# Unread products of constants on TensorE, where it stands idle at the heads of stages, in two routers and behind a recurrence

## The chip, the core and the metric

The kernel runs on one core of a Trainium2 chip. The core has a matrix engine (TensorE, written PE in the profile, with PEld for its weight loads), a vector engine (VectorE, DVE), an activation engine (ScalarE, ACT), GpSimd (POOL) and a queue engine (SyncE, SP) that issues most transfers from the chip's main memory. The metric is device time of one execution in microseconds (us); a kernel's time is the median of its runs. TensorE's clock has two levels, 1.2 and 2.4 GHz; the profile gives the level granted in a stretch as a share of the full one (0.50 and 1.00).

## The reference

A network of eight stages works on 256 tokens of width 1024 (and, in the first three stages, on 256 more of a context), all in 32-bit floats:

```
l0   even_mixer: state-space scan + convolution branch, over 512 rows
m0   moe over 512 rows: sigmoid(t @ router_w), best group of 4 experts, best 2 in it,
     sum over experts of weight * (silu(t @ wg) * (t @ wu)) @ wd
hg   odd_mixer: gated linear recurrence in both directions, then rmsnorm * silu(gate), @ w_out
m1   moe over 256 rows
f0   rmsnorm, ffn: (silu(h @ w_gate) * (h @ w_up)) @ w_down
hy   hybrid of attention and a second gated recurrence
f1   two ffn
nsa  sparse attention
f3   ffn, final rmsnorm
```

In stages l0 to m1 the norm of each stage's input is scaled and shifted by `modulation(cond) = silu(cond) @ w + b`; from f0 on it has a gain alone. The change touches nothing that is computed: what it adds is written to a bank of PSUM that nothing reads.

## The kernel before

**Products.** Every matrix product with weights is made of three TensorE products on halves of the operands (`mm3`, L289 to L291): high by high, high by low, low by high. The weights come from memory as f32 (L456); ScalarE writes their rounded high half (L497), VectorE the rest (L498). A product of unrounded f32 operands ("plain f32") is one instruction in the program and two records in the trace.

**Head of a stage.** The rows are tokens, 128 to a tile. `normed` makes the root mean square from the sums of squares (L315, L333, then three Newton steps at L296 to L300) and scales the rows, even tiles on ScalarE (L379), odd ones on VectorE (L377). `turn` then transposes them on TensorE, 128 columns at a time (L392, one record each), into PSUM banks that VectorE (L413, L399) and ScalarE (L411, L398) empty, and the halves are made there too (L415, L416). Then come the stage's first L289. While the norm is made, TensorE has nothing to do. In f0, hy, f1, nsa and f3 the gain can be put in later, so that `turn` works on the rows before they are scaled; these six heads (f1 has two) are short.

**Router.** The turned rows are multiplied by the router's columns (L1156, then L1161 gathers the parts), ScalarE takes a tanh (L1163), and VectorE ranks the experts in some twenty small instructions, down to the mask of the chosen ones (L1190). TensorE counts each token's place in its expert with a triangle of ones (L1208 to L1210); VectorE makes rows of zeros and ones from the places (L1346 in m0, L1494 in m1), and TensorE turns these into lists of token numbers (m0: L1349, on which a gather by DMA and its transposes at L1363 follow) or multiplies with them (m1: L1501). In m0 TensorE also transposes the rows back for the gather's source (L1284); ScalarE (L1288) and VectorE (L1286) copy them.

**Between m0 and hg.** The last experts' outputs are sent back to their tokens by products (L1456), a bank each; VectorE takes each bank times a gate (L1458) and adds it to the row (L1459), eight times; ScalarE squares the rows (L315), and the head of hg begins.

**End of hg.** After the last products of the gate's projection come eight products of the modulation (L582), which need their weights alone. The last of the recurrence's results are normed and multiplied by the gate on VectorE (L1695), turned (L392), and multiplied by the output weights.

**First stage.** `first_parts` transposes all rows (L680), then the modulation's first part (L562, L567) gives scale and shift, which ScalarE and VectorE apply (L693) ahead of the first L289.

**What sets the order.** The program is traced once; a scheduler in the framework puts each engine's instructions in one list, by the traced order shifted by priorities (`high_priority`, offset up to 9 times `PRIO` = 3000) and by added edges (`issue_after`). Each engine then runs its list in order; an instruction whose operand or bank isn't ready holds all those behind it on its engine. PSUM banks come from pools that a stage opens (`banks=`): a new tile waits until the last reader of the bank that it gets is done, also when that reader belongs to the stage before.

Of the kernel before, what the change touches and what calls it, by code (L numbers as in the profile page):

```python
# [24 lines left out]
P = 128  # L25
# [38 lines left out]
HALF_HY = 5  # L64

# [113 lines left out]
class Ctx:  # L179
# [106 lines left out]
    def mm3(self, out, a, b, first, last):  # L286

        nc = self.nc
        nc.tensor.matmul(out, a[0], b[0], start=first, stop=False)  # L289
        nc.tensor.matmul(out, a[0], b[1], start=False, stop=False)  # L290
        nc.tensor.matmul(out, a[1], b[0], start=False, stop=last)  # L291
# [91 lines left out]
    def turn(self, xn, segs, hi, lo, full=None, of=0):  # L383
# [5 lines left out]
        for k in range(xn[0].shape[1] // P):  # L389
            ps = self.bank(of)  # L390
            for t in range(len(xn)):
                nc.tensor.transpose(ps[:, t * P:(t + 1) * P], xn[t][:, k * P:(k + 1) * P], self.ident)  # L392
# [258 lines left out]
def even_mixer(S, l, gains, X):  # L651
# [19 lines left out]
    with S.tc.manual_schedule(engines={nc.tensor.engine, nc.scalar.engine, V.engine}):  # L671
# [15 lines left out]
        next(firsts[1])  # L687
        for k, wh, wl in collect(W, KT):
            V.tensor_scalar(sc[:, :, k], S.mcol[0][:, 0, k], 1.0, gains[:, k:k + 1], op0=OP.add, op1=OP.mult)
            c, v, sh = plain[k][:, 0:256], plain[k][:, 256:512], S.mcol[0][:, 1, k]  # L690
            nc.scalar.activation(c, c, AF.Identity, scale=sc[:, 1, k:k + 1], bias=sh[:, 1:2])
            V.tensor_scalar(v, v, sc[:, 0, k:k + 1], sh[:, 0:1], op0=OP.mult, op1=OP.add)
            last = nc.scalar.activation(hT[0][k], plain[k], AF.Copy), V.tensor_sub(hT[1][k], plain[k], hT[0][k].bitcast(FT))  # L693
            for f in range(4):
                if f == BEF[k > 0]:
                    for g in firsts[k + 2:k + 3] + firsts[k + 1:k + 2]:
                        next(g)
                fs = slice(f * P, (f + 1) * P)
                S.mm3(four[f], (wh[:, fs], wl[:, fs]), (hT[0][k], hT[1][k]), k == 0, k == KT - 1)
# [444 lines left out]
def route(S, w, hf, nt, room):  # L1144
# [18 lines left out]
    scored = nc.scalar.activation(sc, ps[:, :nt * 16].rearrange("p (t e) -> p t e", e=16), AF.Tanh, scale=0.5)  # L1163
    sel = T("r_sel", nt, 4, 4)
# [45 lines left out]
    nc.tensor.matmul(ps[:, 64:80], S.ones, past[:, nt], start=False, stop=True)  # L1210
# [49 lines left out]
def route_all(S, w, X, segs, room):  # L1260
# [3 lines left out]
    nt = len(X)  # L1264
    xn = S.normed(X, w, known=True)
# [11 lines left out]
    else:  # L1277
        H = S.dram_pool.tile([nt * P, D], FT, name="tokens")
        for t in range(nt):
            h = S.page()  # L1280
            for q in range(2):
                ps = S.bank(1)
                for k in range(4):
                    nc.tensor.transpose(ps[:, k * P:(k + 1) * P], hf[4 * q + k][:, t * P:(t + 1) * P], S.ident)  # L1284
# [4 lines left out]
            nc.gpsimd.dma_start(H[t * P:(t + 1) * P], h)  # L1289
    return hf, H, aux, pos, sc, count  # L1290
# [34 lines left out]
def moe_wide(S, X, segs, gates):  # L1325
# [6 lines left out]
    with ExitStack() as st:  # L1332
# [117 lines left out]
        for t in range(nt):  # L1450
            for q in range(2):
                v = slice(q * 512, q * 512 + 512)
                b = S.bank(1 if t < 2 else 0)
                for i in range(2):
                    for j, y in enumerate(ys[i]):
                        nc.tensor.matmul(b, back[i][:, t * P:(t + 1) * P], y[:, v], start=i + j == 0, stop=i + j == 2)  # L1456
# [19 lines left out]
def moe_narrow(S, X, scale, shift, gates, beside):  # L1476
# [5 lines left out]
    with ExitStack() as st:  # L1482
# [58 lines left out]
        def down(e, act, a, back):  # L1541
# [15 lines left out]
            for t in range(nt):  # L1557
                for j in range(2):
                    for h, r in enumerate((lo, hi)):
                        nc.tensor.matmul(sums[t][h], back[r, t * P:(t + 1) * P], y[j][r], start=e + j == 0, stop=e == 15 and j == 1)  # L1560
# [63 lines left out]
def odd_mixer(S, xin, sc, sh):  # L1624
# [5 lines left out]
    hT = [Rows(S, 8, 512, FR) for _ in range(2)]  # L1630
    S.norm_T(xin, [(0, 2, sc[:, 1], sh[:, 1], None), (2, 2, sc[:, 0], sh[:, 0], "to")], *hT, known=True)
# [51 lines left out]
    for q in range(2):  # L1683
# [6 lines left out]
        if q == 0 and not ORDER:  # L1690
            recur(*last)
    oT = [Rows(S, 8, 256, FR) for _ in range(2)]
# [103 lines left out]
def ffn(S, xs, g, idx, first=None):  # L1796
# [6 lines left out]
    with ExitStack() as st:  # L1803
        w = S.work("ffn", st)
        if first:
# [3 lines left out]
            g = both  # L1809
        S.turn(xs, [(0, nt, g, None, None)], *hT)  # L1810
        if first:
# [101 lines left out]
def hybrid_mixer(S, x, g, name):  # L1913
# [5 lines left out]
    hT = [Rows(S, 8, 256, FR) for _ in range(2)]  # L1919
    S.turn(x, [(0, 2, g, None, None)], *hT)  # L1920
    rr = S.rstd(w, x)
# [239 lines left out]
def sparse_mixer(S, x, g, name):  # L2161
# [6 lines left out]
    hT = [Rows(S, 8, 256, FR) for _ in range(2)]  # L2168
    S.turn(x, [(0, 2, g, None, None)], *hT)
    rr = S.rstd(w, x)  # L2170
# [387 lines left out]
```

## Time and profile before

| | us |
|---|---|
| median of three runs | 2569.3 (2567.41 to 2569.53) |
| the profiled execution | 2571.33 |
| its span, first to last instruction | 2569.5 |
| TensorE busy in the span | 2391.0 (93%) |
| VectorE, ScalarE busy | 1566.4 (61%), 1264.5 (49%) |
| mean granted clock of TensorE | 0.968 |

The profile's page gives busy time by engine, the span in 40 slices with the granted clock, and the chain of waits that ended last. Three views of the trace are used beside it: the timeline (start, duration, engine, line, operation, operands, number of records; in brackets the idle time ahead of them and what ended it), the table of stretches (busy time and number of records of each engine between two moments, with the granted clock), and the granted clock of the whole span. Records of products on TensorE overlap, so that a product's pace is read from one start to the next, not from its duration.

### The profile page before, as it was taken

How to read it: one execution, taken by the hardware profiler on the slowest of the kernel's cores; microseconds unless marked ns; L12 is line 12 of the kernel's file. 1: busy time of each engine (PE TensorE's matmuls, PEld its weight loads, DVE VectorE, ACT ScalarE, POOL GpSimd, SP SyncE). 2: the span in 40 equal slices, each digit the busy share in tenths (PEclk: the TensorE clock that was granted, in tenths of full speed). 3: DMA queues.
4: the chain of work that ended last, by engine and by line, in shares of the span. 5: the costliest groups of instructions: out<-in, count | busy, mean ns of one | idle time of the engine just before them, and what ended most of it. 6: DMA issues, size and time to landing. Idle time of an engine off the chain costs nothing.

```text
span 2569.5 us, 31206 instructions
## 1 busy us (share of the span) xinstructions
PE 2391.0 (93%) x11991; PEld 1744.9 (68%) x11991; DVE 1566.4 (61%) x2519; ACT 1264.5 (49%) x2020; POOL 87.8 (3%) x103
## 2 busy tenths in 40 slices
PE   7999999889999599987999899998999999989998
PEld 5677776666666477765433478776788787756786
DVE  4999997678888826674111455456555554655554
ACT  5358654357777435553211344365444444546442
POOL 0000000011210300000000000000000000000000
PEclk9999999989999799998999999999999999989999
DMA  6552243479999444346999755333555553402552
GB/s 264 193 202 99 83 144 118 163 255 332 364 362 351 155 150 162 116 167 253 381 376 420 292 176 176 123 123 138 190 180 180 180 180 139 171 23 85 206 177 81
DMA packets 78054, 509.48 MB, mean 198 GB/s; under 512 B 9776, under 2 KB 10412, under 8 KB 21571
## 3 DMA queue, kind: packets, MB, share of 16 engines
q1 hardware_dynamic: 73603, 494.13, 52.5%
q0 software_dynamic: 4288, 13.21, 1.6%
q8 instruction: 97, 1.59, 0.2%
q14 instruction: 66, 0.54, 0.1%
HBM read 496.18 MB, written 12.87 MB: 198 GB/s over the span
## 4 chain that ended last, share of the span: by engine, by line
PE 46%; DVE 4%; ACT 3%; issue 1%; DVEq 0%; ACTq 0%
PE ps L289 11%; PE ps L291 11%; PE ps L290 11%; PE ps L1535 5%; PE ps L1552 2%; DVE wl L498 1%; PE ps L1831 1%; ACT wh L497 1%; DVE a L1828 1%; PE ps L1501 1%; PE ps L2281 1%; PE ps L1560 1%; PE ps L2317 0%; ACT pg L2292 0%; DVE ey L1555 0%
## 5 line engine op out<-in xcount | busy, mean ns | idle before, releaser
L498 DVE TENSOR_TENSOR wl<-raw,wh 128x1024 fp32r<-128x1024 f32 x618 | 748.7, 1224 | 497.8 <-ACT wh L497 494.4
L497 ACT ACTIVATE wh<-raw 128x1024 fp32r<-128x1024 f32 x618 | 640.4, 1053 | 576.9 <-PE ps L291 477.6
L289 PE MATMUL ps<-wh,pg 128*128 128x512 f32 (+2 forms) x1596 | 620.0, 389 | 17.4 <-DVE pg L399 6.1
L290 PE MATMUL ps<-wl,pg 128*128 128x512 f32 (+2 forms) x1596 | 613.9, 385 | 1.2 <-DVE wl L498 1.2
L291 PE MATMUL ps<-wh,pg 128*128 128x512 f32 (+2 forms) x1596 | 614.2, 385 | 0.0
L289 PEld LDWEIGHTS ps<-wh,pg 128*128 128x128 f32 x1596 | 303.0, 190 | 84.0 <-DVE pg L399 7.4
L291 PEld LDWEIGHTS ps<-wh,pg 128*128 128x128 f32 x1596 | 303.3, 190 | 62.3 <-issue 4.6
L290 PEld LDWEIGHTS ps<-wl,pg 128*128 128x128 f32 x1596 | 303.6, 190 | 58.9 <-DVE wl L498 2.1
L289 PE MATMUL ps<-pg,wh 128*128 128x512 f32 (+3 forms) x528 | 205.2, 389 | 2.9 <-ACT pg L693 2.9
L290 PE MATMUL ps<-pg,wh 128*128 128x512 f32 (+3 forms) x528 | 201.1, 381 | 0.5 <-DVE pg L693 0.5
L291 PE MATMUL ps<-pg,wl 128*128 128x512 f32 (+3 forms) x528 | 201.3, 381 | 0.0
L823 DVE SCALAR_TENSOR_TENSOR x<-pg,vecs,x 128x512 f32<-128x512 f32 x240 | 171.6, 748 | 2.6 <-ACT x L808 0.4
L1535 PE MATMUL ps<-raw,pg 128*64 128x512 f32 x512 | 131.6, 606 | 0.0
L289 PEld LDWEIGHTS ps<-pg,wh 128*128 128x128 f32 (+2 forms) x528 | 98.4, 186 | 42.0 <-issue 13.8
L291 PEld LDWEIGHTS ps<-pg,wl 128*128 128x128 f32 (+2 forms) x528 | 98.5, 187 | 22.5 <-issue 3.5
L290 PEld LDWEIGHTS ps<-pg,wh 128*128 128x128 f32 (+2 forms) x528 | 98.6, 187 | 19.1 <-DVE pg L693 1.1
L290 PE MATMUL ps<-wl,xe 128*96 128x512 f32 x256 | 104.3, 407 | 1.2 <-DVE wl L498 1.2
L289 PE MATMUL ps<-wh,xe 128*96 128x512 f32 x256 | 102.6, 401 | 0.0
L291 PE MATMUL ps<-wh,xe 128*96 128x512 f32 x256 | 102.5, 400 | 0.0
L1538 DVE TENSOR_TENSOR act<-act,ps 64x512 f32<-64x512 f32 x16 | 10.9, 679 | 128.9 <-ACT act L1537 128.9
L1535 PEld LDWEIGHTS ps<-raw,pg 128*64 128x64 f32 x512 | 38.4, 139 | 65.1 <-issue 62.7
L1552 PE MATMUL ps<-raw,eT 128*64 128x512 f32 x256 | 69.5, 596 | 0.0
(609 smaller groups left out, 2839.3 us busy)
## 6 DMA issues: line engine op xcount, KB each, us to landing
raw<-in_moe_w_up SPq DMA_DIRECT2D x64, 1024.0 KB, 7.4
raw<-in_moe_w_gate SPq DMA_DIRECT2D x64, 1024.0 KB, 8.6
raw<-in_moe_w_down SPq DMA_DIRECT2D x64, 1024.0 KB, 7.9
raw<-in_ffn_w_gate SPq DMA_DIRECT2D x44, 1024.0 KB, 5.0
raw<-in_ffn_w_up SPq DMA_DIRECT2D x44, 1024.0 KB, 4.9
raw<-in_ffn_w_down SPq DMA_DIRECT2D x44, 1024.0 KB, 4.9
raw<-in_mod_w SPq DMA_DIRECT2D x40, 1024.0 KB, 4.8
raw<-in_ab_w_in SPq DMA_DIRECT2D x20, 1024.0 KB, 5.0
```

Of the source, the lines that this page charges most:

```text
L289: nc.tensor.matmul(out, a[0], b[0], start=first, stop=False)
L290: nc.tensor.matmul(out, a[0], b[1], start=False, stop=False)
L291: nc.tensor.matmul(out, a[1], b[0], start=False, stop=last)
L497: nc.scalar.activation(hv, r, AF.Copy)
L498: nc.vector.tensor_sub(lv, r, hv.bitcast(FT))
L823: V.scalar_tensor_tensor(y3, u[:, :, j:j + 64], cfw[:, c, j:j + 1], y3, op0=OP.mult, op1=OP.add)
L1501: nc.tensor.matmul(ps[:, k * 256:(k + 1) * 256], H[i // nt][t][:, (2 * q + k) * P:(2 * q + k + 1) * P], p[:, t, :, 0], start=i == 0, stop= ...
L1535: nc.tensor.matmul(b[r], xe[kk][:, sv], W[:, k * 512:k * 512 + 512], start=kk == 0, stop=kk == KT - 1)
L1552: nc.tensor.matmul(b[r], aT[:, k], W[:, k * 512:k * 512 + 512], start=k == 0, stop=k == 3)
L1560: nc.tensor.matmul(sums[t][h], back[r, t * P:(t + 1) * P], y[j][r], start=e + j == 0, stop=e == 15 and j == 1)
L1828: V.scalar_tensor_tensor(a, up[t][:, :cn], r[t], a, op0=OP.mult, op1=OP.mult)
L1831: nc.tensor.transpose(ps[:, f * P:(f + 1) * P], a[:, f * P:(f + 1) * P], S.ident)
```

## The change

A helper `warm(n)` issues n plain f32 products of two constant tables, 128x128 by 128x256, into a PSUM bank that nothing reads. An edge puts them behind a given TensorE instruction (`behind`, or the last of the helpers that now note it in `self.last`), a priority ahead of the rest. It is called at the heads of m0 (20 products), hg (60), m1 (22) and the six short heads (3 ahead of the transposes, 6 behind them), behind the routers' first products (24 and 18), behind the counts (4 and 6), and at the end of hg ahead of its transposes (25). Nine more are written out in the first stage. That makes 242 products.

```
+WARM = {("head", 4): 20, ("route", 4): 24, ("placed", 4): 4, "hg": 60, "hg end": 25, ("head", 2): 22, ("route", 2): 18, ("placed", 2): 6, "ffn": 3,
+        "turned": 6}
...
-        nc.tensor.matmul(out, a[1], b[0], start=False, stop=last)
+        self.last = nc.tensor.matmul(out, a[1], b[0], start=False, stop=last)
+
+    def warm(self, n, of=0, behind=None):
+        if not n:
+            return
+        ps, ones = self.bank(of), self.squares[:, 1:3].rearrange("p i c -> p (i c)")
+        with self.tc.high_priority(offset=PRIO), self.tc.issue_after((behind or self.last).ins):
+            for _ in range(n):
+                self.nc.tensor.matmul(ps[:, :256], self.ident, ones, start=True, stop=True)
...
         next(firsts[1])
+        ps = S.bank(1)
+        for _ in range(9):
+            nc.tensor.matmul(ps[:, :256], S.ident, S.squares[:, 1:3].rearrange("p i c -> p (i c)"), start=True, stop=True)
         for k, wh, wl in collect(W, KT):
...
     scored = nc.scalar.activation(sc, ps[:, :nt * 16].rearrange("p (t e) -> p t e", e=16), AF.Tanh, scale=0.5)
+    if nt == 2:
+        S.warm(WARM["route", nt], behind=found)
...
-    nc.tensor.matmul(ps[:, 64:80], S.ones, past[:, nt], start=False, stop=True)
+    S.warm(WARM["placed", nt], behind=nc.tensor.matmul(ps[:, 64:80], S.ones, past[:, nt], start=False, stop=True))
...
     nt = len(X)
+    S.warm(WARM["head", nt])
     xn = S.normed(X, w, known=True)
...
             nc.gpsimd.dma_start(H[t * P:(t + 1) * P], h)
+        S.warm(WARM["route", nt], 1)
...
     hT = [Rows(S, 8, 512, FR) for _ in range(2)]
+    S.warm(WARM["hg"])
     S.norm_T(xin, [(0, 2, sc[:, 1], sh[:, 1], None), (2, 2, sc[:, 0], sh[:, 0], "to")], *hT, known=True)
...
             recur(*last)
+    S.warm(WARM["hg end"])
     oT = [Rows(S, 8, 256, FR) for _ in range(2)]
...
+        S.warm(WARM["ffn"])
         S.turn(xs, [(0, nt, g, None, None)], *hT)
+        S.warm(WARM["turned"])
```

The last hunk stands in `ffn` and, alike, in the stages hy and nsa. The transposes of `turn` and of the router, and the products that send rows back, note themselves in `S.last` too. The lines below the helper move by 12, later ones by 15 to 27: L392 is L404 after the change, L1284 L1302, L1208 L1225, L1456 L1475, L582 L594. The helper's product is L303.

TensorE's list from the last product of m0 to the head of hg. Before (`pg` are rows and parts of them, `ps` banks, `squares` the constant tables):

```order
L1456 MATMUL ps_10672<-pg_10537,pg_10357 128x512
L1456 MATMUL ps_10672<-pg_10538,pg_10357 128x512
L392 MATMUL ps_10746<-squares,pg_10734 128x128
L392 MATMUL ps_10746<-squares,pg_10735 128x128
L392 MATMUL ps_10746<-squares,pg_10736 128x128
```

and now:

```order
L1475 MATMUL ps_10733<-pg_10599,pg_10418 128x512
L303 MATMUL ps_10780<-squares 128x256 x60
L404 MATMUL ps_10868<-squares,pg_10856 128x128
L404 MATMUL ps_10868<-squares,pg_10857 128x128
L404 MATMUL ps_10868<-squares,pg_10858 128x128
```

The 60 products stand between the last L1475 (L1456 before) and the first of 32 transposes. The bank that they write, `ps_10780`, lies where the seventh of the eight banks of L1475, `ps_10723`, lay: the first of them waits until VectorE has read that one (L1477, L1458 before).

TensorE's list in the router of m0, from the last transposes back to the token lists. Before:

```order
L1284 MATMUL ps_4276<-squares,pg_4095 128x128 x2
L1284 MATMUL ps_4276<-squares,pg_4096 128x128 x2
L1208 MATMUL ps_4213<-r_mk_4195,squares 128x64
L1209 MATMUL ps_4213<-r_past_4207,ones 128x64
L1210 MATMUL ps_4213<-r_past_4207,ones 128x16
L1349 MATMUL ps_4288<-r_aux_4202,pe_4283 96x4 x4
```

and now:

```order
L1302 MATMUL ps_4312<-squares,pg_4126 128x128 x2
L1302 MATMUL ps_4312<-squares,pg_4127 128x128 x2
L303 MATMUL ps_4319<-squares 128x256 x24
L1225 MATMUL ps_4244<-r_mk_4226,squares 128x64
L1226 MATMUL ps_4244<-r_past_4238,ones 128x64
L1227 MATMUL ps_4244<-r_past_4238,ones 128x16
L303 MATMUL ps_4248<-squares 128x256 x4
L1368 MATMUL ps_4349<-r_aux_4233,pe_4344 96x4 x4
```

The 24 stand ahead of the counts, the four between the counts and the lists. The first of the 24 waits for a copy of ScalarE (L1306, L1288 before) out of the bank that it gets.

TensorE's list at the end of hg. Before:

```order
L291 MATMUL ps_12716<-wh_12769,pg_10718 128x512
L582 MATMUL ps_11942<-raw_12870,cond 32x512 x4
L582 MATMUL ps_11942<-raw_12876,cond 32x512 x4
L392 MATMUL ps_12829<-squares,pg_11103 128x128
L392 MATMUL ps_12834<-squares,pg_11103 128x128
L392 MATMUL ps_12839<-squares,pg_11103 128x128
```

and now:

```order
L293 MATMUL ps_12838<-wh_12891,pg_10779 128x512
L303 MATMUL ps_12911<-squares 128x256 x25
L404 MATMUL ps_12977<-squares,pg_11225 128x128
L404 MATMUL ps_12977<-squares,pg_11226 128x128
L404 MATMUL ps_12982<-squares,pg_11225 128x128
L404 MATMUL ps_12982<-squares,pg_11226 128x128
L404 MATMUL ps_12987<-squares,pg_11225 128x128
L404 MATMUL ps_12987<-squares,pg_11226 128x128
L404 MATMUL ps_12992<-squares,pg_11225 128x128
L404 MATMUL ps_12992<-squares,pg_11226 128x128
L594 MATMUL ps_12064<-raw_13018,cond 32x512
L404 MATMUL ps_12997<-squares,pg_11225 128x128
```

The 25 stand where the modulation's products stood, right behind the gate's projection; their bank's last reader is done by then. The eight products of the modulation (L594, L582 before) now stand among the transposes, one ahead of the ninth and the others behind the fourteenth and the sixteenth. The lists of GpSimd and SyncE are what they were; those of VectorE and ScalarE move one weight's halves in the router of m0.

## Rows read from the trace of the kernel before

**Rows 1.** Which engine is busy, and the granted clock in 40 slices (the page)
```profile
PE 2391.0 (93%) x11991; PEld 1744.9 (68%) x11991; DVE 1566.4 (61%) x2519; ACT 1264.5 (49%) x2020; POOL 87.8 (3%) x103
...
PEclk9999999989999799998999999999999999989999
```

**Rows 2.** The chain that ended last, by engine (the page)
```profile
PE 46%; DVE 4%; ACT 3%; issue 1%; DVEq 0%; ACTq 0%
```

**Rows 3.** Stretches of the span (the first line names the columns)
```profile
core 0: us, PE busy (x) PEld busy (x) DVE busy (x) ACT busy (x) POOL busy (x), PEclk, DMA share, GB/s
...
28.10:31.60 3.50, 3.50 (x15) 2.03 (x17) 0.69 (x1) 0.34 (x1) 0.00 (x0) 0.51 1.00 404
...
526.00:530.00 4.00, 4.00 (x10) 2.61 (x11) 1.05 (x3) 1.44 (x2) 0.72 (x1) 0.51 0.67 198
...
871.20:884.20 13.00, 0.00 (x0) 0.00 (x0) 12.33 (x37) 6.24 (x15) 0.00 (x0) 0.50 0.24 81
884.20:888.30 4.10, 4.05 (x18) 3.73 (x19) 2.65 (x7) 4.07 (x7) 0.00 (x0) 0.50 0.00 0
...
892.00:1138.00 246.00, 244.94 (x1462) 193.49 (x1460) 136.85 (x206) 125.22 (x186) 3.77 (x12) 1.00 0.39 142
...
1154.30:1158.00 3.70, 3.68 (x10) 2.91 (x11) 0.24 (x2) 0.27 (x1) 0.57 (x1) 0.51 1.01 418
...
1197.90:1205.70 7.80, 5.99 (x24) 5.14 (x26) 4.09 (x17) 1.78 (x4) 0.00 (x0) 0.50 0.03 6
```

**Rows 4.** Timeline of TensorE, a plain f32 product: start, busy us, line, shape, records, idle before
```profile
338.47 0.60 PE L1032 MATMUL ps<-pg,half 128*128 128x256 f32 x2
338.90 0.61 PE L1052 MATMUL ps<-pg,pg 128*128 128x128 f32 x4
```

**Rows 5.** Timeline around the head of hg
```profile
876.86 0.68 DVE L1458 TENSOR_TENSOR pg<-ps,pg 128x512 f32<-128x512 f32 x1
...
884.25 5.33 PE L392 MATMUL ps<-squares,pg 128*128 128x128 f32 x28 [16.69 <-ACT pg L379]
...
891.16 0.50 PE L289 MATMUL ps<-wh,pg 128*128 128x512 f32 x1 [0.71 <-ACT pg L411]
```

**Rows 6.** Timeline of TensorE, head and router of m0
```profile
488.06 0.28 PE L432 MATMUL ps<-squares,mcol 128*8 128x128 f32 x1 [1.11 <-DVE pg L783]
493.61 6.40 PE L392 MATMUL ps<-squares,pg 128*128 128x128 f32 x31 [5.27 <-ACT pg L379]
...
506.10 1.94 PE L1284 MATMUL ps<-squares,pg 128*128 128x128 f32 x16
514.35 0.69 PE L1208 MATMUL ps<-r_mk,squares 128*128 128x64 f32 x2 [6.30 <-DVE r_mk L1190]
...
518.64 2.35 PE L1349 MATMUL ps<-r_aux,pe 128*96 128x4 f32 x12 [1.43 <-DVE pe L1346]
...
524.34 1.51 PE L1363 MATMUL ps<-squares,xg 96*128 96x96 f32 x8 [1.58 <-DMA xg<-tokens,ix]
```

**Rows 7.** Timeline of TensorE, end of hg
```profile
1138.21 1.92 PE L582 MATMUL ps<-raw,cond 128*32 128x512 f32 x16
1146.70 1.12 PE L392 MATMUL ps<-squares,pg 128*128 128x128 f32 x4 [6.57 <-DVE pg L1695]
```

**Rows 8.** Timeline of TensorE, head and router of m1
```profile
1184.22 1.12 PE L392 MATMUL ps<-squares,pg 128*128 128x128 f32 x4 [6.13 <-ACT pg L379]
...
1197.93 0.61 PE L1208 MATMUL ps<-r_mk,squares 128*128 128x32 f32 x2 [4.84 <-DVE r_mk L1190]
...
1201.14 3.75 PE L1501 MATMUL ps<-pe,pg 128*128 128x256 f32 x16 [1.78 <-DVE pe L1494]
```

**Rows 9.** Timeline of TensorE, first stage
```profile
26.13 0.50 PE L289 MATMUL ps<-pg,wh 128*128 128x512 f32 x1 [2.54 <-ACT pg L693]
```

**Rows 10.** Stretches at two of the six small heads
```profile
1661.30:1666.50 5.20, 5.20 (x15) 4.78 (x16) 2.59 (x10) 2.76 (x8) 0.00 (x0) 0.50 0.34 102
1785.00:1787.00 2.00, 0.62 (x6) 0.39 (x5) 2.00 (x4) 2.00 (x7) 0.00 (x0) 1.00 0.00 0
```

More of the change, by code (lines that the diff above doesn't have):

```diff
@@ L391, in turn @@
             for t in range(len(xn)):
-                nc.tensor.transpose(ps[:, t * P:(t + 1) * P], xn[t][:, k * P:(k + 1) * P], self.ident)
+                self.last = nc.tensor.transpose(ps[:, t * P:(t + 1) * P], xn[t][:, k * P:(k + 1) * P], self.ident)
             if segs[0][3] is None and full is None:
@@ L1283, in route_all @@
                 for k in range(4):
-                    nc.tensor.transpose(ps[:, k * P:(k + 1) * P], hf[4 * q + k][:, t * P:(t + 1) * P], S.ident)
+                    S.last = nc.tensor.transpose(ps[:, k * P:(k + 1) * P], hf[4 * q + k][:, t * P:(t + 1) * P], S.ident)
                 if q:
@@ L1455, in moe_wide @@
                     for j, y in enumerate(ys[i]):
-                        nc.tensor.matmul(b, back[i][:, t * P:(t + 1) * P], y[:, v], start=i + j == 0, stop=i + j == 2)
+                        S.last = nc.tensor.matmul(b, back[i][:, t * P:(t + 1) * P], y[:, v], start=i + j == 0, stop=i + j == 2)
                 tmp = S.page()[:, :512]
@@ L1559, in down @@
                     for h, r in enumerate((lo, hi)):
-                        nc.tensor.matmul(sums[t][h], back[r, t * P:(t + 1) * P], y[j][r], start=e + j == 0, stop=e == 15 and j == 1)
+                        S.last = nc.tensor.matmul(sums[t][h], back[r, t * P:(t + 1) * P], y[j][r], start=e + j == 0, stop=e == 15 and j == 1)
             yield
@@ L1919, in hybrid_mixer @@
     hT = [Rows(S, 8, 256, FR) for _ in range(2)]
+    S.warm(WARM["ffn"])
     S.turn(x, [(0, 2, g, None, None)], *hT)
+    S.warm(WARM["turned"])
     rr = S.rstd(w, x)
@@ L2168, in sparse_mixer @@
     hT = [Rows(S, 8, 256, FR) for _ in range(2)]
+    S.warm(WARM["ffn"])
     S.turn(x, [(0, 2, g, None, None)], *hT)
+    S.warm(WARM["turned"])
     rr = S.rstd(w, x)
```

## The prediction

> **What bounds the kernel now.** I read the page first: TensorE is busy 93% of the span, and the clock line has four slices under 9 tenths [rows 1]. The chain that ended last gives TensorE 46% and every other engine 4% or less [rows 2]. So what shortens TensorE's list shortens the kernel, and what lengthens it lengthens it, except where it waits. Then the table of stretches, at the places of the change [rows 3]: the reader is to see that the clock is at 0.50 in stretches that follow an idle one, at the ends of gaps of 5 to 17 us, and that the 246 us of hg behind its head are full: 244.94 us busy at 1.00. Last the timelines of the heads and routers [rows 5 to 8], for when each gap ends and what ended it. With a mean clock of 0.968 some 3% of the span, 82 us, are lost to the half clock; but part of that is idle, and a good part lies where the change adds nothing.
>
> **The price of one unread product.** The same shape in the same type, 128*128 128x256 f32, stands at L1032: one product leaves two records, and from its start at 338.47 to the next start 0.43 us pass [rows 4]. Twice that, 0.86 us, at half the clock. The count of two records holds for plain f32 elsewhere: L1208 is one instruction in the list and two records [rows 6, 8]. So 242 products are 104 us of TensorE at full clock; each group is priced by where its start is held, its length, and when the next instruction is ready.
>
> **Head of hg (60).** The rows are ready for the transposes at 884.25, after 16.69 us idle. The products cannot start at the idle time's beginning: their bank is free when the seventh of eight gate products on VectorE is done, 876.86 + 0.68 = 877.54 [rows 5]. By then the clock is at 0.50 (from 871.20 on) [rows 3]. In the kernel before it rose 4.05 us after TensorE had set to work again (884.25 to 888.30); with the same lag 4.7 products run at 0.86 us and 55.3 at 0.43: 877.54 + 4.05 + 23.8 = 905.4. The transposes begin 21.1 us late. At full clock they win back at most half of 4.05 us; VectorE and ScalarE, which empty the banks, allow about 1.5. So +19.6 (18 to 21). Nothing behind swallows it: to 1138 TensorE is full [rows 3]. What it hides is small: the weights' halves get further ahead, and no wait for them is in the stretch. If the bank did not bind, the products would run from 867.56 (884.25 − 16.69) to 893.4, and the cost would be +7 to +9.
>
> Here the Trainium skill has a rule (TensorE: Matmul & The Clock Gate, Part 4: PE-mode transpose): the full clock does not engage for transposes, which do not count as busy. The rows differ: from 884.20 to 888.30 TensorE ran transposes alone, and the next stretch was at full clock. By the rule the first weight products of hg would have paid about 4 us at half clock before, the unread products would save 2 us more, and the sum would be some 2 us lower; the measurement decides, so I leave that out.
>
> **Head and router of m0 (20, 24, 4).** TensorE's last L432 starts at 488.06 [rows 6]; the products follow VectorE's read of a bank at about 488.6, and 20 × 0.43 end at 497.2, 3.6 us behind the transposes' old start of 493.61. These went at half clock, 31 in 6.3 us (0.20 each); at full clock L1284 has 16 in 1.94 (0.12) [rows 6], so 2.5 come back and the rest about comes back in the products behind: 0. The 24 begin when the transposes back (L1284, until about 508) and a copy out of their bank are done, and last 10.3 us, to about 518.3. The mask is ready for L1208 at 514.35: +4.0 there. Four more products stand ahead of L1349 (1.7 us, against an idle 1.43). Counts and lists run at full clock, so that L1349 is about 2 us late, and the gather, whose L1363 came at 524.34, with it. If the clock then holds over the wait for the gather, the stretch 526 to 530 (at 0.51) gives 2 us back; TensorE idles there once more, and in the idle time ahead of 884.25 the clock did fall, so that I count less than half. Sum +1.2 (−2 to +3).
>
> **End of hg (25).** These start when the gate's projection ends, at 1138.2, and end at 1148.9, 2.2 us behind the transposes' old start of 1146.70 [rows 7]. The 1.92 us of the modulation's products, which ran in that gap [rows 7], go among the transposes, where TensorE waits for banks. Against it the half clock to 1158 goes: 1154.3 to 1158 was full at 0.51 [rows 3], worth 1.8, and the transposes make up the delay. −1.5 (−3 to +2.2).
>
> **Head and router of m1 (22, 18, 6).** From 1178.1 (1184.22 − 6.13) the 22 last to 1187.6, 3.4 late; transposes and router products to the mask, at half clock before, make up nearly all of it. The 18 (7.7 us) start at about 1193.2 and end at 1200.9, where the mask was ready at 1197.93: +3.0. The six (2.6) put L1501 at 1204.0 instead of 1201.14 [rows 8]. L1501's first 16 records took 3.75 us at 0.50 [rows 3, 8]; at full clock they take half. Sum +1.3 (0 to +2.9).
>
> **First stage (9) and six short heads (54).** Nine are 3.9 us in a gap of 2.54 ahead of 26.13 [rows 9]: +1.3, and the stretch 28.1 to 31.6 at 0.51 [rows 3] gives 1.7 back: −0.5 (−1.7 to +1.3). A short head gets 3 + 6 = 3.9 us. Where the clock had not fallen it is all cost: 1785 to 1787 had 1.38 us idle at 1.00 [rows 10], so up to +2.5; I take +1.2, since the six run while banks are being emptied. Where it had fallen (1661.3 to 1666.5 at 0.50, full, worth 2.6 [rows 10]) it is about −0.8. Three heads are of each kind: +1 (−5 to +8).
>
> **The sum**: 19.6 + 1.2 − 1.5 + 1.3 − 0.5 + 1 = +21.1, on the profiled execution's 2571.3, is 2592.4. That execution is 2.0 above the median of the runs, so the forecast is 2590.
>
> **Rivals.**
> (a) *Half the price, and the change wins.* If an unread product cost one record (0.21 us), the head of hg would still end about 8 us late (4.05 + 55.3 × 0.21 = 15.7 behind 877.54, so 893.2 against 884.25; +6.5 behind the transposes' gain), but every other group would fit its gap: m0 −3, end of hg −3, m1 −2.5, first stage −1.5, short heads −5. That is −8.5: 2561. Between the two prices (+21.1 at 0.43, −8.5 at 0.21) the sum is zero at about 0.27 us a product. For it speaks that the half clock does follow the gaps [rows 3]; against it L1032 [rows 4]. The Trainium skill's rule (TensorE: Matmul & The Clock Gate, Why this matters for your kernels) leans to this side: it wants no longer idle gaps between bursts of products, or the clock goes back to its lower level. Not slower; chance 0.11.
> (b) *The bank at hg does not bind*, or the counts fall otherwise between engines: +7 to +9 there instead of 19.6: 2578 (2573 to 2584). Against it speaks the list, in which the bank is that of the seventh of eight. Chance 0.12.
> (c) *Cost without the gain*: the clock falls all the same, in the waits that are left (the gather, the mask, the empty banks), and what I counted as given back, about 10 us in all, is not: 2600 (2595 to 2606). For it: the products end before the stage's work is dense again; against it: they end at the very instruction that waits. Chance 0.10.
> The change may also do nothing that can be measured (gains and costs within 5 us of each other): 0.05.
>
> **How the numbers follow.** The forecast has 0.62, its own range is 2583 to 2597. About 0.2% (5 us) is what a measurement of this kernel can tell from no change, so faster means under 2564, slower over 2574.5. Faster: (a), and a little of the short heads: 0.12. Same: 0.05 and the low edge of (b): 0.06. Slower: 0.82. The range from 2566 to 2599 leaves out most of (a) and half of (c), under 2 in 10.
>
> **What will show it.** In the profile after: L303 with two records for each product and a pace of 0.43 us; its first record in hg at 877 to 878, the first transpose there at about 905, the first L291 (L289 before) near 911; full clock from about 882 on; 24 products that end at about 518 in m0, with the counts at once behind them; the end of hg and the first stage a little earlier in their own stretch. The prediction is wrong if a product's pace is under 0.3 us, if the transposes of hg begin before 895, or if TensorE behind that head has waits that give the delay back.

## The result and the profile after

| | median us | of before, 95% interval |
|---|---|---|
| before, beside it | 2569.4 | 1 |
| the change | 2608.5 (2607.5 to 2609.8) | 1.0158 (1.0145 to 1.0171) |

The change makes the kernel 39 us slower. The sign was forecast, the size not: 2590 was predicted, and 2608.5 lies beyond the range's end at 2599.

The page of the changed kernel, as in [rows 1]: busy time by engine, the granted clock in 40 slices, and the chain that ended last, by line.

```profile
PE 2477.9 (95%) x12475; PEld 1825.8 (70%) x12475; DVE 1566.2 (60%) x2519; ACT 1263.5 (48%) x2020; POOL 87.8 (3%) x103
...
PEclk9999999989999899999999999999999999999999
...
PE ps L291 10%; PE ps L293 10%; PE ps L292 10%; PE ps L1554 5%; PE ps L1571 2%; DVE wl L510 1%; PE ps L1854 1%; ACT wh L509 1%; PE ps L303 1%; PE ps L1520 1%; DVE a L1851 1%; PE ps L1579 1%; PE ps L2308 0%; PE ps L2344 0%; ACT pg L2319 0%
```

TensorE is busy 86.9 us more (2391.0 before), and the clock is full in more slices: its mean went from 0.968 to 0.980. The unread products do raise the clock (over the executions here it is 0.963 to 0.968 before and 0.980 to 0.981 after); the span is 37.9 us longer all the same (2607.4), and L303 stands in the chain with 1%.

The line of the unread products: records, duration (least, median, most) and shapes, then who ended the idle time ahead of them.

```profile
L303 PE MATMUL ps<-squares x466: 377/379/796, 490.7 to 2406.6; 128*128 128x256 f32 x156
...
  DVE pg L1477: 20.4, 2
  DVE pg L411: 6.8, 8
```

These are 466 records, two to each of 233 products; the nine in the first stage are written out on another line and have the other 18 of the 484. The group at hg waits for L1477, which is L1458 of before, as forecast. (The idle times in this view count TensorE and its weight loads, so that each wait stands in them twice.) L411 (L399 before) is VectorE's emptying of the banks at the short heads: that row holds the largest error of the prediction, as will be seen.

**The head of hg**, the timeline of TensorE, answers to [rows 5]:

```profile
877.81 28.11 PE L303 MATMUL ps<-squares 128*128 128x256 f32 x120 [9.98 <-DVE pg L1477]
905.75 3.33 PE L404 MATMUL ps<-squares,pg 128*128 128x128 f32 x28
...
912.06 0.50 PE L291 MATMUL ps<-wh,pg 128*128 128x512 f32 x1
...
913.16 0.63 PE L291 MATMUL ps<-wh,pg 128*128 128x512 f32 x1
```

The 60 products start at 877.81 (877.54 was forecast) and hold the list until 905.7 (905.4). The first L291 (L289 before) starts at 912.06, 20.9 us later than in [rows 5]. From the first transpose to that product 6.3 us pass, 6.9 in the kernel before. The same stretch in the table, with the columns of [rows 3]:

```profile
877.80:881.80 4.00, 3.99 (x10) 3.20 (x11) 3.50 (x13) 2.79 (x7) 0.00 (x0) 0.50 0.00 0
881.80:905.70 23.90, 23.90 (x112) 21.04 (x111) 3.53 (x18) 3.22 (x7) 0.00 (x0) 1.00 0.00 1
905.70:912.00 6.30, 3.91 (x33) 3.38 (x31) 3.20 (x6) 3.72 (x7) 0.00 (x0) 1.00 0.00 0
912.00:916.00 4.00, 4.00 (x12) 3.15 (x11) 2.20 (x4) 2.70 (x7) 0.00 (x0) 0.57 0.00 0
```

The clock is up at 881.8, as forecast, and stays up to 912.5. Then it falls again, for 3.4 us, just as the weight products begin: between 905.7 and 912.0 TensorE was busy 3.91 of 6.30 us, with transposes that wait for banks to be emptied. So the first weight products run at half clock after all (0.43 us from one start to the next instead of 0.23), which adds 1.4. Behind it TensorE is full, as in [rows 3], and the delay passes through.

**A short head**, that of f1's first ffn. The timeline before:

```profile
1783.54 1.97 PE L392 MATMUL ps<-squares,x 128*128 128x128 f32 x16
...
1786.35 3.23 DVE L399 SCALAR_TENSOR_TENSOR pg<-ps,vecs,pg 128x256 fp32r<-128x256 f32 x8
...
1786.89 0.50 PE L289 MATMUL ps<-wh,pg 128*128 128x512 f32 x1 [1.38 <-DVE pg L399]
```

and after:

```profile
1814.66 1.56 PE L303 MATMUL ps<-squares 128*128 128x256 f32 x6
...
1816.06 1.91 PE L404 MATMUL ps<-squares,x 128*128 128x128 f32 x16
...
1817.47 3.22 DVE L411 SCALAR_TENSOR_TENSOR pg<-ps,vecs,pg 128x256 fp32r<-128x256 f32 x8
...
1818.00 2.86 PE L303 MATMUL ps<-squares 128*128 128x256 f32 x12
...
1820.51 0.58 PE L291 MATMUL ps<-wh,pg 128*128 128x512 f32 x1
```

Before, TensorE is done with its transposes at 1785.5 and waits 1.38 us for VectorE, whose first emptying of a bank (L399) starts at 1786.35, since it works on a weight's low half until then. After, six of the products (12 records) start when the first emptying is done, 1818.00, and the weight products follow at 1820.51, 2.5 us later. The stage's eight banks hold the eight transposed column groups: the ninth tile, that of the products, must wait for the same emptied bank as the first weight product. So the six don't fill the idle time; they start where it ends. The three ahead of the transposes do fill it: they take 1.40 us, the transposes now end at 1817.97, and the step over this head, 2.6 us, is the length of the six.

In hy the clock had fallen as well by the time that they could start (at half from 1687.3 to 1694.1), and the six take 4.7 us:

```profile
1680.42 1.46 PE L303 MATMUL ps<-squares 128*128 128x256 f32 x6
...
1689.61 5.08 PE L303 MATMUL ps<-squares 128*128 128x256 f32 x12 [0.66 <-DVE pg L411]
1694.34 0.54 PE L291 MATMUL ps<-wh,pg 128*128 128x432 f32 x1
```

**The end of hg**, answering to [rows 7]:

```profile
1175.60 1.06 PE L594 MATMUL ps<-raw,cond 128*32 128x512 f32 x6
1177.36 1.06 PE L601 MATMUL ps<-vecs,pg 128*128 128x8 f32 x8 [0.71 <-ACT pg L598]
...
1178.74 0.77 PE L291 MATMUL ps<-wh,pg 128*128 128x512 f32 x1
...
1179.73 0.63 PE L293 MATMUL ps<-wh,pg 128*128 128x512 f32 x1
```

The last of the modulation's products (L594) now run at 1175.60, ScalarE's copy of them ends a wait of 0.71 us ahead of L601, and L601 stands ahead of the first L291 in the list. That one starts at 1178.74, 24.4 us behind the start of the same stretch in [rows 3], where the delay ahead of the place was 22.6. Two products further the start is 1179.73: the clock is at half again, from 1178.7 to 1182.1.

**Head and router of m1**, answering to [rows 8]:

```profile
1218.47 8.02 PE L303 MATMUL ps<-squares 128*128 128x256 f32 x36
1226.32 0.30 PE L1225 MATMUL ps<-r_mk,squares 128*128 128x32 f32 x2
...
1229.39 2.27 PE L1520 MATMUL ps<-pe,pg 128*128 128x256 f32 x16
```

All of it at full clock now, and later: L1225 comes 28.4 us behind L1208 of [rows 8], the first L1520 28.3 behind L1501.

By the difference between the starts of the same product in both traces, ahead of and behind each place, the profiled executions' 37.9 us come from:

| place | forecast | measured step |
|---|---|---|
| first stage | −0.5 | −0.4 |
| l0, the rest; m0 to the end of its experts | 0; +1.2 | +2.4; −1.7 |
| head of hg | +19.6 | +22.0 |
| end of hg | −1.5 | +1.7 |
| m1, to the end of its experts | +1.3 | +2.7 |
| six short heads (0.7 in f0, 3.0 hy, 2.6 and 2.5 f1, 1.0 nsa, 2.6 f3) | +1 | +12.4 |
| elsewhere (hg +0.3, hy +0.4, nsa −1.9) | 0 | −1.2 |

In m0 the head and the router alone give +2.1; the rest, −3.8, lies behind, among the experts, where no product was added. A step in a place that the change doesn't touch can be the clock's: in l0 it fell at a gap that is the same in both traces. The table of stretches there, before and then after:

```profile
439.30:442.00 2.70, 0.05 (x2) 0.02 (x1) 2.70 (x5) 2.70 (x5) 0.00 (x0) 1.00 0.28 114
442.00:448.00 6.00, 6.00 (x26) 4.97 (x27) 6.00 (x10) 6.00 (x11) 0.00 (x0) 1.00 0.44 137
```

```profile
439.50:442.20 2.70, 0.05 (x1) 0.00 (x0) 2.70 (x5) 2.70 (x5) 0.00 (x0) 0.86 0.27 111
442.20:448.30 6.10, 6.10 (x14) 4.79 (x15) 6.10 (x10) 6.10 (x11) 0.00 (x0) 0.50 0.44 129
```

With TensorE idle 2.65 us in both, the 6 us behind it went at 1.00 in one and at 0.50 in the other. Run 1 below, whose program is that of the change up to here, kept 1.00.

### The profile page after: what moved, and what is told of

Same layout as the page of the kernel before. It is cut to its first block, busy times and chain, and to the rows that moved or that the text cites. A ratio compares the mean times of both kernels' runs of the same rounds, so it can differ in the third digit from the quotient of the medians.

```text
span 2607.4 us, 32166 instructions
## 1 busy us (share of the span) xinstructions
PE 2477.9 (95%) x12475; PEld 1825.8 (70%) x12475; DVE 1566.2 (60%) x2519; ACT 1263.5 (48%) x2020; POOL 87.8 (3%) x103
## 4 chain that ended last, share of the span: by engine, by line
PE 46%; DVE 3%; ACT 3%; issue 1%; DVEq 0%; ACTq 0%
PE ps L291 10%; PE ps L293 10%; PE ps L292 10%; PE ps L1554 5%; PE ps L1571 2%; DVE wl L510 1%; PE ps L1854 1%; ACT wh L509 1%; PE ps L303 1%; PE ps L1520 1%; DVE a L1851 1%; PE ps L1579 1%; PE ps L2308 0%; PE ps L2344 0%; ACT pg L2319 0%
## 5 line engine op out<-in xcount | busy, mean ns | idle before, releaser
L291 PE MATMUL ps<-wh,pg 128*128 128x512 f32 (+2 forms) x1596 | 619.8, 389 | 7.5 <-ACT wh L509 3.2
L291 PEld LDWEIGHTS ps<-wh,pg 128*128 128x128 f32 x1596 | 303.0, 190 | 71.9 <-ACT wh L509 4.7
L291 PE MATMUL ps<-pg,wh 128*128 128x512 f32 (+3 forms) x528 | 204.7, 388 | 0.4 <-ACT pg L708 0.4
L291 PEld LDWEIGHTS ps<-pg,wh 128*128 128x128 f32 (+2 forms) x528 | 98.3, 186 | 39.2 <-issue 13.8
L303 PE MATMUL ps<-squares 128*128 128x256 f32 x466 | 110.9, 396 | 13.2 <-DVE pg L1477 10.0
L303 PEld LDWEIGHTS ps<-squares 128*128 128x128 f32 x466 | 91.3, 199 | 29.5 <-DVE pg L1477 10.4
L291 PE MATMUL ps<-wh,xe 128*96 128x512 f32 x256 | 102.7, 401 | 0.0
```

The costliest lines, as they stand in the source:

```text
L303: self.nc.tensor.matmul(ps[:, :256], self.ident, ones, start=True, stop=True)
```

## The experiments

Each run is set against executions of the kernel before on the same chip (medians from 2567.6 to 2570.8 us); ratios are to these. The chips differ, so a ratio is the better measure between two runs. A *step* is read from a trace, as in the table above: by how much TensorE's delay against the kernel before grows over a place.

**1. Without the group at the head of hg.**

```
-"hg": 60, "hg end": 25
+"hg": 0, "hg end": 25
```

> The change without the 60 products at the head of hg; the other 182 stay. Theory 1 (each group costs the part of its own length that stands over the idle time it was put in, and TensorE passes that on to the end): the trace of the changed kernel shows TensorE 22.0 us later behind the head of hg than ahead of it, so 2608.5 - 22.0 = 2586.5 us (2584 to 2589). Theory 2 (a good part of the 22 is the clock, which falls again behind the late head, from 912.5 to 915.9 us, and would fall without the products as well): the head is again at half clock from its idle time, and the time is 2590 or more.

Measured: 2584.4 us, ratio 1.0051 (1.0035 to 1.0066), 24 us under the change (27.5 by the ratios). Theory 1 holds: this one group is 60 to 70% of the loss.

**2. The short heads alone.** All other groups left out.

```
-WARM = {("head", 4): 20, ... "turned": 6}
+WARM = {("head", 4): 0, ... "hg": 0, "hg end": 0, ... "ffn": 3, "turned": 6}
-        for _ in range(9):
+        for _ in range(0):
```

> The kernel before with the 3 + 6 products at the six short heads alone (54 of the 242). The prediction had +1 us for them, so 2570.4. Theory 1, by the steps of TensorE's delay in the trace of the changed kernel (0.7 in f0, 3.05 in hy, 2.6 and 2.6 in f1, 1.0 in nsa, 2.6 in f3): +12.5, so 2582 (2580 to 2584). Theory 2 (the steps there hang on where the clock happened to fall in that execution, not on the products): 2570 to 2577.

Measured: 2580.2 us, 1.0046 (1.0032 to 1.0061): +10.4, or +11.8 by the ratio. In its trace the steps at hy, f1 and f3 come again within 0.3 us (3.3, 2.6, 2.5, 2.6; nsa 1.0), while f0 is 0.7 faster. Theory 1 holds, and the prediction's +1 is refuted.

**3. Half the length.**

```
-        ps, ones = self.bank(of), self.squares[:, 1:3].rearrange("p i c -> p (i c)")
+        ps, ones = self.bank(of), self.squares[:, 1]
-                self.nc.tensor.matmul(ps[:, :256], self.ident, ones, start=True, stop=True)
+                self.nc.tensor.matmul(ps[:, :128], self.ident, ones, start=True, stop=True)
```

> The change with products of 128 columns instead of 256, so that each is half as long (0.21 us at full clock), the counts the same. Theory 1: the head of hg still ends late (877.5 us, 4.05 us at half clock with 9.4 products, then 50.6 at 0.215: 892.5 against 884.25, less 1.5 from the transposes: +6.7); the short heads lose the three products ahead of the transposes (+0.6 each, +3 in all with hy); the rest fits its gaps and gains about 4: +5, so 2575 (2571 to 2580). The prediction's rival (a) had -8.5, so 2561.

Measured: 2575.1 us, 1.0021 (1.0008 to 1.0033), the time that theory 1 had, but not by its parts: the head of hg cost 11.0 (6.7 expected), and the first stage, m0 and m1 gave back 9.4 (about 4 expected). Even at half the price the change doesn't win. Rival (a) had a wrong price, since products of the full length take 0.43; of its gains those in the first stage, m0 and m1 came (−1.6, −3.1, −4.7), and those at the end of hg (+0.6) and at the short heads (+3.1 together) didn't.

**4. Counts that fit the gaps.**

```
+WARM = {("head", 4): 11, ("route", 4): 8, ("placed", 4): 0, "hg": 37, "hg end": 14, ("head", 2): 13, ("route", 2): 10, ("placed", 2): 3, "ffn": 0, "turned": 3}
...
-        for _ in range(9):
+        for _ in range(5):
...
+        S.warm(WARM["hg"], 1)      # at the end of moe_wide, behind the loop of L1456
...
-    S.warm(WARM["hg"])
```

> The change with counts that fit the idle times at 0.43 us a product: 5 in the first stage, 11, 8 and 0 in m0, 37 at the head of hg (in a bank of m0's, read long before, so that they start when m0's last product is done), 14 at the end of hg, 13, 10 and 3 in m1, and at the short heads none ahead of the transposes and 3 behind them. Theory 1: no group ends after its gap, the clock is full at the heads, and the time falls to 2563 (2559 to 2567), with the half clock gone from 871 to 888 and from 1144 to 1206. Theory 2 (the clock that is won at the heads is lost again at other places, or the heads are bound by the emptying of the banks, not by TensorE): 2568 to 2572.

Measured: 2571.4 us, 1.0002 (0.9991 to 1.0013): no gain; the time is theory 2's. Theory 1 as I had it, that a group which fits its gap is free, is refuted. At three short heads (both of f1, and f3) the three products behind the transposes cost 1.3 us each time, though at the first of f1 TensorE had 1.38 idle; at the others the step is +0.5 (hy), −0.3 (nsa) and −1.6 (f0). At the head of hg the step is +1.3. And at the end of hg the clock did not last. The table of stretches there (length; busy us and records of PE, PEld, DVE, ACT, POOL; granted clock; DMA):

```profile
1138.00:1146.60 8.60, 8.12 (x45) 5.57 (x44) 8.57 (x31) 1.72 (x3) 0.00 (x0) 1.00 0.07 9
1146.60:1149.60 3.00, 1.55 (x10) 1.04 (x10) 2.07 (x6) 1.28 (x4) 0.00 (x0) 1.00 0.90 358
1149.60:1154.10 4.50, 3.81 (x18) 2.79 (x17) 2.90 (x9) 2.50 (x7) 0.00 (x0) 0.51 1.00 422
1154.10:1156.60 2.50, 2.50 (x7) 2.01 (x8) 0.21 (x2) 0.23 (x1) 0.57 (x1) 0.51 1.03 426
```

To 1146.6 TensorE is nearly full at 1.00, on to 1149.6 it has sparse transposes at 1.00, and from there the clock is at half, into the weight products. What the products kept up is lost again in the sparse stretch between them and the dense work.

**5. Ahead of the transposes or behind them.** Short heads alone, three ahead in f0, hy and f1's first ffn, six behind in f1's second and in nsa, none in f3.

```
+WARM = {... "ahead": (3, 3, 0, 0, 3, 0), "behind": (0, 0, 6, 0, 0, 6)}    # f0, f1, f1, f3, hy, nsa
-        S.warm(WARM["ffn"])
+        S.warm(WARM["ahead"][idx])
-        S.warm(WARM["turned"])
+        S.warm(WARM["behind"][idx])
```

> Products at the short heads alone, in two kinds: 3 ahead of the transposes and none behind in f0, hy and the first ffn of f1; 6 behind and none ahead in the second ffn of f1 and in nsa; none in f3. Read from the trace, as the step of TensorE's delay over each head. Theory 1 (the price is paid behind the transposes, because of the bank): first ffn of f1 0 us (0 to 0.4), second +2.6, f3 0. The prediction's reading (three ahead cost 1.3, six behind half hidden, 1.2): +1.3, +1.2, 0.

Measured, as steps in the trace: first ffn +0.4, second +2.5, nsa +1.0, f3 0.0 (one execution, 2569.2); further f0 −2.6 and hy +2.0. f1's first ffn:

```profile
1778.52 1.56 PE L302 MATMUL ps<-squares 128*128 128x256 f32 x6 [0.78 <-DVE x L646]
...
1779.91 1.91 PE L403 MATMUL ps<-squares,x 128*128 128x128 f32 x16
...
1780.84 3.23 DVE L410 SCALAR_TENSOR_TENSOR pg<-ps,vecs,pg 128x256 fp32r<-128x256 f32 x8
...
1781.58 0.48 PE L290 MATMUL ps<-wh,pg 128*128 128x512 f32 x1
```

The three (six records) stand ahead of the transposes; VectorE's emptying (L410) starts 0.93 us after the first transpose, when it is done with a weight, and the weight product follows that by 0.74 (0.54 before). f1's second:

```profile
1971.44 2.03 PE L403 MATMUL ps<-squares,x 128*128 128x128 f32 x16
...
1973.87 3.22 DVE L410 SCALAR_TENSOR_TENSOR pg<-ps,vecs,pg 128x256 fp32r<-128x256 f32 x8
...
1974.40 2.86 PE L302 MATMUL ps<-squares 128*128 128x256 f32 x12 [0.93 <-DVE pg L410]
...
1976.91 0.58 PE L290 MATMUL ps<-wh,pg 128*128 128x512 f32 x1
```

The six wait 0.93 us for the first emptying, and the weight product comes 2.5 us after their start. Theory 1 holds at the three heads that it names, and against the prediction's reading: what stands ahead of the transposes is nearly free, since VectorE is what the head waits for; what stands behind them costs its whole length, because of the bank. Equal numbers show it too: at f1's first ffn three ahead cost 0.4 here and three behind 1.3 in run 4. The three ahead in hy, at +2.0, don't fit as they stand. There the half clock reached 6.0 us into the weight products; with the same three ahead in run 9 it reached 2.9 us into them, and the step was +0.6.

**6. The fitted counts without the short heads.**

```
-"turned": 3
+"turned": 0
```

> The fitted counts (5; 11, 8, 0; 37 early; 14; 13, 10, 3) without any product at the six short heads. Theory 1 (a product behind a short head's transposes waits for the same emptied bank that the first weight product waits for, so that it fills no idle time and adds its whole 0.43 us): the fitted kernel lost 1.3 us at each of five short heads in its trace, so 2571.4 - 6.5 = 2565 (2562 to 2568), a little faster than the kernel before. Theory 2 (what the fitted groups win is lost again by the clock at other places): 2569 to 2572.

Measured: 2563.8 us, 0.9986 (0.9976 to 0.9995), in theory 1's range: 0.14% faster than the kernel before. The number is partly luck: theory 1 took five heads at 1.3 us for it, and run 4's trace has three; by the ratios the heads' products had cost 4 us, not 6.5.

**7. Sixty products that start early.** They are issued at the end of m0, into a bank of m0's; all others left out.

```
+        S.warm(WARM["hg"], 1)      # at the end of moe_wide, behind the loop of L1456
...
-    S.warm(WARM["hg"])
```

> The 60 products at the head of hg alone, into a bank of m0's that VectorE has read long before, so that they start when m0's last product is done, at about 867.6 us instead of 877.5. The other 182 are left out. Theory 1 (start held by the bank, then 0.43 us each): they end at about 893.4, the delay behind the head is 8 us, the time 2569.8 + 8 = 2578 (2575 to 2581). Against it: if the start doesn't matter since VectorE and ScalarE pace the head, 2590.

Measured: 2577.1 us, 1.0041 (1.0028 to 1.0054), +9.5, as theory 1 had it. They run at full clock from their start (1.00 from 859.9 to 1146.6):

```profile
863.24 26.06 PE L302 MATMUL ps<-squares 128*128 128x256 f32 x120
889.14 3.32 PE L403 MATMUL ps<-squares,pg 128*128 128x128 f32 x28
...
895.42 0.50 PE L290 MATMUL ps<-wh,pg 128*128 128x512 f32 x1
```

25.9 us for 60, at the 0.43 of [rows 4]. The start 10 us earlier takes the group's price from 22 to 27 us down to 9.5 (8.6 as the step in the trace): the bank's hold is more than half of what it cost in the change.

**8. End of hg, the modulation ahead of the products.**

```
+    S.fill(16)                                       # the modulation's last eight, ahead
+    S.warm(WARM["hg end"], behind=S.modlast)         # 20 products, alone in the kernel
```

> Products at the end of hg alone, 20 of them, behind the eight products of the modulation, which keep their old place right behind the gate's projection; they end at the same moment as the 25 of the change (about 1148.9). Read from the trace, as the step of TensorE's delay over the end of hg (it was +1.7 in the changed kernel). Theory 1 (the moved modulation products hold the list back, since L589, which needs their result, stands ahead of the first L289): the step is 0.3 or less. Theory 2 (the late transposes are the cost, and the clock falls again behind them): +1.3 to +2.

Measured, as the step in the trace over the end of hg: −1.4 right behind it, −0.7 from 1160.4 on, where TensorE waits 0.41 us for a weight's low half (+1.7 in the change).

```profile
1134.83 1.92 PE L593 MATMUL ps<-raw,cond 128*32 128x512 f32 x16
1137.47 0.39 PE L600 MATMUL ps<-vecs,pg 128*128 128x8 f32 x2 [0.72 <-ACT pg L597]
1137.72 8.88 PE L302 MATMUL ps<-squares 128*128 128x256 f32 x40
...
1151.27 0.50 PE L290 MATMUL ps<-wh,pg 128*128 128x512 f32 x1 [0.28 <-ACT row L445]
```

The modulation's wait (0.72, L600) now lies ahead of the products, where TensorE is idle anyway, and the clock was full from 885.8 on, right through the weight products. The step is within theory 1's bound. Against the delay ahead of the place the first weight product is 0.3 us late here and 1.8 in the change; so 1.5 lie in the list, 0.71 of them the wait, and the rest is the half clock behind it, which the change had and this run hadn't. But that the order saves 3.1 us, or that the 20 products gain, isn't shown: traces with no product at this place have steps of −0.6, −2.5, +0.6 and +1.4 there (runs 2, 5, 7, 11), as the half clock falls.

**9. The change without the head of hg and without the six behind.**

```
-"hg": 60, ... "turned": 6
+"hg": 0, ... "turned": 0
```

> The change without the 60 products at the head of hg and without the six behind the transposes of each short head (146 products stay). Theory 1: by the steps in the traces so far, the six behind cost 1.8 in f0, 1.0 in hy, 2.2 and 2.6 in f1, 1.0 in nsa and 2.6 in f3 beyond the three ahead, 11.2 in all; against 2584.4 without hg's alone that is 2573 (2570 to 2576). Theory 2 (the three ahead share the cost evenly, by their length): 2584.4 - 8 = 2576.5 or more.

Measured: 2570.9 us, 1.0007 (0.9996 to 1.0019), 13.5 us under run 1 (11 by the ratios), within theory 1's range. The two edits take nearly all of the change's 39 us away. In the trace the three that are left ahead of the transposes have steps of −1.8 in f0, +0.6 in hy, +0.4 and 0.0 in f1, −1.6 in nsa and 0.0 in f3.

**10. All that paid, together.** Counts as in run 6, the end of hg as in run 8 (14 products), three ahead in f0.

```
-        S.warm(WARM["ffn"])
+        S.warm(3 if idx == 0 else 0)
-    S.warm(WARM["hg end"])
+    S.fill(16)
+    S.warm(WARM["hg end"], behind=S.modlast)
```

> The fitted counts without the short heads, as in the run that was 0.9986 of before, and two edits: the 14 products at the end of hg stand behind the modulation's eight, which keep their place, and f0 has three ahead of its transposes (a step of -2.6 there in the trace of the two kinds). Theory 1: 1 to 3 us under the 2563.8 of that run, 2561.5, ratio 0.998. Theory 2 (these steps were the clock of one execution): 2564, ratio 0.9986.

Measured: 2557.4 us, 0.9956 (0.9941 to 0.9971), more than I had expected. It beats both kernels. Of the 8 us under run 6 (by the ratios) the trace shows 2.6 at f0; the end of hg has the step of run 6 (−0.4 and −0.6), and where the rest comes from isn't shown. At the head of hg its table of stretches shows what is left of the idea there:

```profile
860.50:876.60 16.10, 16.10 (x75) 13.85 (x73) 15.33 (x45) 9.40 (x19) 0.00 (x0) 1.00 0.21 66
877.40:884.50 7.10, 4.49 (x33) 3.69 (x34) 4.15 (x9) 6.01 (x12) 0.00 (x0) 1.00 0.00 0
884.50:888.20 3.70, 3.70 (x10) 2.86 (x10) 2.20 (x4) 2.40 (x6) 0.00 (x0) 0.54 0.00 0
```

37 products at full clock in the gap, transposes (busy 4.49 of 7.10 us) at full clock, and half clock again for the first weight products. TensorE's delay grows by 1.4 us over this head, against the kernel before.

**11. The same without any product in hg.**

```
-"hg": 37, "hg end": 14
+"hg": 0, "hg end": 0
```

> The last kernel (ratio 0.9956) without any product in hg: neither the 37 early ones at its head nor the 14 at its end; 5 in the first stage, 11 and 8 in m0, 13, 10 and 3 in m1 and 3 in f0 stay. Theory 1 (the head of hg is paced by VectorE and ScalarE, which empty the banks, and the clock falls again in the sparse transposes behind the products, so that even fitted products win nothing there: a step of +1.35 in that kernel's trace): the ratio is the same or lower, 0.995 to 0.996. Theory 2 (filling the longest gap of the kernel is where the gain is): 0.997 to 0.999.

Measured: 2557.5 us, 0.9953 (0.9937 to 0.9968). Theory 1 holds: within these intervals the 51 products in hg win nothing, fitted as they are. The gain of 0.47% (0.32 to 0.63) is in m0, m1, the first stage and f0, with 53 products where the change has 242. No run takes these four apart, but the steps of the traces so far do:

| place | no product there | as many as in the change | fitted |
|---|---|---|---|
| first stage | 0.0 to +0.7 (runs 2, 5, 7, 8) | −0.9 (9 products) | −1.6 (5; runs 4, 6, 10, 11) |
| m0, head and router | −1.3 to −0.1 (2, 5, 7, 8) | +2.1 to +2.8 (48) | −3.1 to −2.3 (19; 4, 6, 10, 11) |
| head of hg | −0.4 to +0.8 (1, 2, 5, 8, 9, 11) | +22 (60) | +1.3 to +3.2 (37; 4, 6, 10) |
| m1, head and router | −0.4 to +0.7 (2, 5, 7, 8) | +1.7 to +4.5 (46) | −4.7, once −3.0 (26; 4, 6, 10, 11) |
| f0 | −0.4 to 0.0 (6, 7, 8) | −0.8 to +0.7 (3 and 6) | −2.6, once −1.8 (3 ahead; 5, 10, 11; 9) |

(The third column is the change and the runs with its counts: 1 and 9, for f0 1 and 2. The first stage is taken here from 20 us on; the table of the change counts it from the span's start.) In run 11 the four add up to −11.8 us, against 12.1 by its ratio. So at the same place a fitted group gains where an overlong one loses: in m1 26 products won 4.7 us and 46 lost 2 or more. At the head of hg even the fitted ones cost more than none.

## Why the prediction was wrong

The step that failed is the one on the short heads: "I take +1.2, since the six run while banks are being emptied", for the other kind "about −0.8", and with them "Three heads are of each kind: +1". They are 12.4 of the change's steps, 11.4 more than forecast. The three where the clock had not fallen (f1 twice, f3) cost 7.7, where 3.6 was forecast; the three where it had (f0, hy, nsa) cost 4.7, where −2.4 was. The list and the row were both there: the idle 1.38 us was read as time that the six could use, though the bank they wait for is the one whose emptying ends that idle time (runs 4 and 5). So the six add their whole length, 2.6 us at full clock, and 4.7 in hy, where the clock had fallen when they could start. The upper end, +2.5 a head, was right for the three heads of the first kind, and with its reason, the 3.9 us of all nine less 1.38: the three ahead fill the idle time, and halving the rest was the error.

Right: the sign; the price of 0.43 us; that the bank at hg holds the 60 until the seventh emptying, to 0.3 us; that the head of hg is the largest part of the loss and that nothing behind swallows it; the first stage. None of the three signs of being wrong that the prediction names came. Rival (b)'s price, +7 to +9 for an early start, came out at 8.6 as a step and 9.5 in the median (run 7). Partly luck is the end of the 60 to 0.3 us: it rests on the clock's rising 4.05 us after their start, as it had in the kernel before, and in run 3 it rose 4.9 us after (869.26 to 874.2). Luck too is that l0 (+2.4) and the experts of m0 (−3.8), where no product was added, nearly cancel.

Too low by 2.4 us: the head of hg, 22.0 against 19.6, outside its own range of 18 to 21. The transposes were to win back 1.5 at full clock and won 0.6, since VectorE and ScalarE pace them; and the clock falls behind them (1.4). Wrong in sign, though within its range: the end of hg (−1.5, measured +1.7). The transposes with the modulation's products among them made up 0.4 us of their 2.2 us of delay, the wait at L601 for those products cost 0.71, and the half clock, which was to go, came again; what the order alone costs stays open (run 8). Too low by 1.4: m1. Rival (c) had the nearest time, 2600 (2595 to 2606), and half the cause: behind the wait for the gather in m0, in hg's head, its end, and hy the clock fell again behind the products. Yet it missed the short heads too. Rival (a)'s working keeps 55.3 products behind the lag; at half the price 50.6 are left there, and the head ends at 892.2, which is the 8 us that its sum uses.

The gains, too, were read wrongly from the half clock. Between the two traces the mean clock rose by 0.012, and yet at the head of hg, the longest gap that was filled, fitted products win nothing (runs 10 and 11): from the first transpose to the first weight product 6.9 us passed before, with the clock at half for 4.05 of them, and 6.3, 6.3 and 6.8 at full clock in the change and in runs 7 and 10. That head is paced by the engines that empty the banks, and TensorE's level there matters little.

## What to carry to other kernels

Work that only keeps an engine's clock up is priced like any other work in the list: when it can start (whose bank or buffer it waits for), its length, and what stands behind it. Before filling an idle time, ask whether the filler waits for the event that ends it; if so it fills nothing and adds its whole length. Fit the count to the idle time: in m1 the right number won 4.7 us and nearly twice as many lost 2. And fill only gaps behind which the engine itself is the limit, right up to the dense work: sparse work in between can give the clock back.

## What was not expected of the hardware

The clock is not the same from one execution to the next in the same code: after the same gap of 2.65 us in l0 it was 1.00 in two traces (the kernel before, run 1) and 0.50 in the change, worth 2.8 us right behind the gap and 1.8 by the end of the stage; the kernel before spread from 2563 to 2578 us over its executions here, with mean clocks from 0.968 down to 0.963. So a step of 2 or 3 us in a single trace says little until it has come again in others. And behind unread products that ran at full clock, sparse transposes kept it in one trace (run 7, 889.14 to 895.42) and lost it in others (the change at 912, run 10 at 884.5).
